# Three weight blocks at a time at the start of seven dense layers, identity products in the norms, and a mean taken later

## The chip, the cores and the metric

The kernel runs on one core of a Trainium2 chip. The metric is the time of one execution on the device, in microseconds (us); where several runs are given, their median. The engines are TensorE (PE; its weight loads PEld), VectorE (DVE), ScalarE (ACT), GpSimd (POOL) and SyncE (SP), whose queue issues most of the loads.

## The reference

Three chains of layers are computed one behind the other on 256 tokens of width 1024 (272 rows where the third chain puts 16 extra tokens ahead). Mixers of several kinds (attention, convolution, state-space and recurrent layers) alternate with dense layers. The dense layer around which the change turns is

```python
def macaron_half_ffn(x, pre_g, post_g, w_gate, w_up, w_down):
    h = rmsnorm(x, pre_g)
    h = (jax.nn.silu(h @ w_gate) * (h @ w_up)) @ w_down
    return x + 0.5 * rmsnorm(h, post_g)
```

with inner width 2816. In the second chain the norm behind a layer is a LayerNorm, which needs a mean and a variance over the 1024 features.

## The kernel before

Activations lie transposed: 8 chunks `k` of 128 features by n tokens. A product with weights is made of three fp32r products of 128x128 by n (L594, L595, L596 in `mm3p`): the weights are split in a high part `wh` (cast on ScalarE, L237) and a low part `wl` (subtraction on VectorE, L238), the activations in `xh` (L253 or L270, ScalarE) and `xl` (L254 or L271, VectorE). Weights come in pieces of 128x1024 fp32 (four rows of chunks by 256 columns) through six raw buffers and five buffers each for `wh` and `wl`. A `get` of eight chunks by 256 columns takes two such pieces.

A dense layer (`ffn`) goes over 11 column blocks `c` of 256. For each it takes a gate and an up block of weights, 8 chunks each. In block 0 of a layer that is not the program's first, gate and up run together per chunk k: 12 matmuls for each chunk, so that TensorE can begin with the first chunk of the normalised input. Then `glu`, and `out_proj` with the down weights: 4 column blocks, each over 22 chunks of the inner width in groups of 8, and for each group first one half of the columns (m = 0), then the other (m = 1). `RmsOut` and `LnOut` take the results, square them (ScalarE: L776, L779, L822) and add the squares up (POOL, L363).

A norm is a place where everything depends on the last result. `add_norm` sums the squares over features with TensorE (`tok_sum`, L295, in parts), makes the reciprocal root of 128x2 numbers in small steps (`inv_sqrt`: L336 or L338 on VectorE, L339 on ScalarE, L340 to L343 on VectorE), broadcasts it with TensorE (`bcast`, L325), scales (L794), adds the residual (L795), and the next layer's `split_x` makes `xh` and `xl`. There are 12 such norms. `layer_norm` (4 of them) does the same with two sums (L866 to L869 take the mean off the variance), two broadcasts and L878 to L880. `hold_weights` sets how many further `get`s may be issued before those whose splits are held back behind the root's steps L339 and L343: after `held` gets the next one waits for both.

`LnOut.late` takes the mean of the first 768 features off before the last two chunks are there, so that the squares need no large terms: a product with ones (L851), a copy (L853), and subtractions on POOL (L854, L855) and VectorE (L857). In `out_proj` it is called for the last column block after the first group of the first half, m = 0.

The order of instructions on each engine is set by a scheduler in the build, which places each instruction by the time it expects for it. So where the source adds an instruction, others move too. Side tasks (the next mixer's inputs, for example) run beside some norms; at others nothing else is there for TensorE.

Of the kernel before, what the change touches and what calls it, by code (L numbers as in the profile page):

```python
# [8 lines left out]
F32 = mybir.dt.float32  # L9
# [11 lines left out]
KD = D // 128  # L21
# [150 lines left out]
def parts_tile(p, name, k, n, dtype=F32R, **kw):  # L172

    return p.tile([128, k, (n + 63) // 64 * 64], dtype, name=name, **kw)[:, :, :n]
# [68 lines left out]
class Ops(Net):  # L243
# [49 lines left out]
    def tok_part(self, ps, a, nt, first, last):  # L293
        for j in range(nt):
            self.nc.tensor.matmul(ps[:, j:j + 1], a[:, j * 128:(j + 1) * 128], self.tab["ones"],  # L295
                                  start=(j == 0 and first), stop=(j == nt - 1 and last), skip_group_check=True)

    def rsqrt(self, v, nt, name="rs"):

        nc = self.nc  # L300
        m = self.tiny.tile([128, nt], F32, name=name + "m")
        y = self.tiny.tile([128, nt], F32, name=name + "y")
        t = self.tiny.tile([128, nt], F32, name=name + "t")
        i = self.tiny.tile([128, nt], I32, name=name + "i")
        nc.vector.tensor_scalar(i, v.bitcast(I32), 1, None, op0=OP.logical_shift_right)
        nc.vector.tensor_scalar(y.bitcast(I32), i, -1, 0x5F3759DF, op0=OP.mult, op1=OP.add)
        nc.vector.tensor_scalar(m, v, -0.5, None, op0=OP.mult)
        for _ in range(3):
            nc.vector.tensor_mul(t, y, y)
            nc.vector.tensor_mul(t, t, m)  # L310
            nc.vector.scalar_tensor_tensor(y, t, 1.5, y, op0=OP.add, op1=OP.mult)
        return y
# [205 lines left out]
    def ffn(self, x, n, g, wg, wu, wd, out, first=None, side=None, stats=None):  # L518

        nc = self.nc
        with self.phase("ffn") as p, ExitStack() as scope:
            px = scope.enter_context(self.phase("ffx", side="right"))
            vt = rb = ahead = wide = None
            if first:
                x.need(0)
                parts = []
                for i, (k, m) in enumerate(((0, 2), (2, 2), (4, 4))):
                    parts.append(wg.get(k, m, 0, 256))  # L530
                    x.need(i + 1)
                ahead = [Pieces(2, [t for q in w for t in (q.tiles[0][:, i:i + 2] for i in range(0, q.each, 2))])
                         for w in zip(*parts)]
                first()
            xh, xl = self.split_x(px, x, n, g)
            hh = parts_tile(p, "hh", FF // 128, n)
            hl = parts_tile(p, "hl", FF // 128, n)
            pair = n <= 256

            def tiles(other=0):  # L540
                if pair:
                    t = self.acc.tile([128, 2, 256], F32, name="acc")
                    return t[:, :, :n], [t[:, m, :n] for m in range(2)]
                t = [(self.acc, self.aux)[m < other].tile([128, 512], F32, name=("acc", "aux")[m < other])[:, None, :n]
                     for m in range(2)]
                return t, [a[:, 0] for a in t]

            def mm(ps, w, k):
                for m in range(2):
                    ms = slice(m * 128, m * 128 + 128)  # L550
                    self.mm3p(ps[m], w[0][:, k, ms], w[1][:, k, ms], xh[:, k], xl[:, k],
                              k == 0 and (m == 0 or not pair), k == KD - 1 and (m == 1 or not pair))

            for c in range(FF // 256):
                cg = ahead if ahead and c == 0 else wg.get(0, KD, c * 256, 256)
                cu = wu.get(0, KD, c * 256, 256)
                tg, pg = tiles(2 * (c == 1))
                tu, pu = tiles(c == 1)
                if c == 0 and not first:
                    for k in range(KD):  # L560
                        mm(pg, cg, k)
                        mm(pu, cu, k)
                else:
                    for k in range(KD):
                        mm(pg, cg, k)
                    for k in range(KD):
                        mm(pu, cu, k)
                if c == 0 and g is not None and n == 256 and stats is None:
                    rb, wide = self.rms_wide(p, x, n)
                elif c == 0 and g is not None:  # L570
                    rt, rb, vt = self.rms(x, stats or n)
                    if side:
                        side.stats = rt, rb
                    rb, vt = rb[:, :n], vt[:, :self.nt(n)]
                    if not pair:
                        self.hold_weights(1)
                if pair:
                    self.glu(p, hh[:, 2 * c:2 * c + 2], hl[:, 2 * c:2 * c + 2], tg, tu, rb, n, 2)
                else:
                    for m in range(2):  # L580
                        i = 2 * c + m
                        self.glu(p, hh[:, i:i + 1], hl[:, i:i + 1], tg[m], tu[m], rb, n, 1)
            o = out(hh[:, FF // 128 - 1, 0:1].bitcast(F32))
            self.out_proj(wd, hh, hl, n, list(range(FF // 128)), o, side=side and (lambda: side.place(px)))
            if side:
                side.scope = scope.pop_all()
            if wide is not None:
                vt = self.by_tokens(wide, n, 1e-6)
            return o, vt
# [25 lines left out]
    def out_proj(self, w, hh, hl, n, ks, out, early=None, side=None):  # L615

        blocks = [ks[i:i + 8] for i in range(0, len(ks), 8)]
        for c in range(KD // 2):
            if c == 1 and side:
                side()  # L620
            if early is not None and c < len(early.open):
                early.rest(c, out)
                continue
            pair = n <= 256 and c < KD // 2 - 1
            if pair:
                t = self.acc.tile([128, 2, 256], F32, name="acc")
                ps = [t[:, m, :n] for m in range(2)]
            else:
                t = [self.acc.tile([128, 512], F32, name="acc")[:, None, :n] for _ in range(2)]
                ps = [a[:, 0] for a in t]  # L630
            for bi, b in enumerate(blocks):
                k0 = min(b)
                assert sorted(b) == list(range(k0, k0 + len(b)))
                wt = w.get(k0, len(b), c * 256, 256)
                for m in range(2):
                    ms = slice(m * 128, m * 128 + 128)
                    for kk, k in enumerate(b):
                        self.mm3p(ps[m], wt[0][:, k - k0, ms], wt[1][:, k - k0, ms], hh[:, k], hl[:, k],
                                  bi == 0 and kk == 0 and (m == 0 or not pair),
                                  bi == len(blocks) - 1 and kk == len(b) - 1 and (m == 1 or not pair))  # L640
                    if bi == 0 and m == 0 and c == KD // 2 - 1 and len(blocks) > 1 and isinstance(out, LnOut):
                        out.late()
                    if bi == len(blocks) - 1 and not pair:
                        out.evac(2 * c + m, t[m])
            if pair:
                out.evac(2 * c, t[:, :, :n])
# [113 lines left out]
class RmsOut:  # L760
# [23 lines left out]
    def add_norm(self, x, g, half, vt, last=False):  # L784
        s, nc, n = self.s, self.s.nc, self.n
        ss = s.tok_sum([self.total[0], self.last], n)
        c, _ = s.inv_sqrt(ss, s.nt(n), 1.0 / D, 1e-6 if vt is None else vt, half)
        s.hold_weights()
        cb = s.bcast(c, n)
        xn = s.xp.tile([128, KD, n], F32, name="x")  # L790

        def make(k):
            t = s.tmp.tile([128, n], F32, name="t")
            nc.vector.scalar_tensor_tensor(t, self.o[:, k], s.col(g, k), cb, op0=OP.mult, op1=OP.mult)  # L794
            (nc.gpsimd if last and k % 2 else nc.vector).tensor_add(xn[:, k], x[:, k, :n], t)  # L795

        return Lazy(xn, make)


class LnOut:  # L800
# [59 lines left out]
    def layer_norm(self, g, b, width=None):  # L860
        s, nc, n, o = self.s, self.s.nc, self.n, self.o
        nt = s.nt(n)
        m1 = s.tok_sum([o[:, 6], o[:, 7]], n)
        s2 = s.tok_sum([self.sum2[0]] + self.squares, n)
        v0, m, mm, mr = (s.tiny.tile([128, nt], F32, name="ln" + k) for k in "0123")
        nc.vector.tensor_scalar(m, m1, 1.0 / D, None, op0=OP.mult)  # L866
        nc.vector.tensor_mul(mm, m, m)
# [2 lines left out]
        r, _ = s.inv_sqrt(v0, nt, 1.0, 0.0)  # L870
# [1727 lines left out]
```

## Time and profile before

| | |
|---|---|
| median of 3 runs | 3132.03 us (3131.13 to 3134.92) |
| profiled execution | 3120.05 us |
| its span, first to last instruction | 3117.8 us |
| TensorE busy | 3009.0 us, 97% |
| VectorE busy | 2071.4 us, 66% |
| ScalarE busy | 1527.8 us, 49% |
| POOL busy | 324.1 us, 10% |
| data read from memory | 487.35 MB, 157 GB/s over the span |

The busy time of TensorE counts matmuls at whatever clock was granted. The rows further down show single places: a timeline row gives when an instruction (or a run of the same ones) started, how long it lasted, its engine and line, what it writes and reads, and in brackets how long the engine was idle before it and what ended that.

### The profile page before, as it was taken

To read this page: it belongs to the slowest core of one execution; us is meant where nothing else is said; L and a number is where in the kernel's file an instruction comes from. 1 tells how busy PE (TensorE), PEld (TensorE's weight loads), DVE (VectorE), ACT (ScalarE), POOL (GpSimd) and SP (SyncE) were. 2 spreads that over 40 slices of the span, in tenths; PEclk is the share of its full clock that TensorE was granted. 3 is DMA by queue.
4 is the path that set the end of the run, shared out by engine and by line. 5 is a ranking of instruction groups with operands and counts; after the bars stand their busy time and mean duration, and the time that the engine had idled before them with its cause. 6 is when DMAs were issued, how large, how long until landed. Compare 5 with 4: busy or idle time off the path is not lost.

```text
span 3117.8 us, 63347 instructions
## 1 busy us (share of the span) xinstructions
PE 3009.0 (97%) x26260; PEld 2899.6 (93%) x26260; DVE 2071.4 (66%) x3465; ACT 1527.8 (49%) x2418; POOL 324.1 (10%) x379
## 2 busy tenths in 40 slices
PE   8999999999899999999999999999999999999998
PEld 8998999999777899999989999999989999998898
DVE  6578766658867765657886665565566656658764
ACT  5455555545433544546565454454444444444543
POOL 0010101000211100001100110100102001012101
PEclk9999999999999999999999999999999999999999
DMA  7664566665311466765345536555443555662453
GB/s 241 192 190 137 167 188 191 203 201 172 103 36 35 123 192 197 208 191 174 112 135 161 171 118 194 180 155 171 142 129 108 172 170 165 193 196 90 130 192 119
DMA packets 142528, 494.61 MB, mean 159 GB/s; under 512 B 15760, under 2 KB 18448, under 8 KB 141984
## 3 DMA queue, kind: packets, MB, share of 16 engines
q1 hardware_dynamic: 136512, 478.88, 49.8%
q10 hardware_dynamic: 5696, 11.62, 1.1%
q8 instruction: 206, 3.38, 0.4%
q14 instruction: 82, 0.67, 0.1%
q0 software_dynamic: 32, 0.07, 0.0%
HBM read 487.35 MB, written 3.15 MB: 157 GB/s over the span
## 4 chain that ended last, share of the span: by engine, by line
PE 90%; DVE 5%; ACT 2%; POOL 2%; issue 1%; DMA 0%; SPq 0%; POOLq 0%; DVEq 0%; ACTq 0%
PE acc L594 25%; PE acc L595 25%; PE acc L596 25%; PE aux L1430 2%; DVE wl L238 1%; PE aux L295 1%; POOL acc L363 1%; PE aux L325 1%; PE acc L2433 1%; ACT wh L237 1%; PE acc L514 1%; PE acc L515 1%; PE acc L516 1%; PE aux L1450 0%; PE aux L668 0%
## 5 line engine op out<-in xcount | busy, mean ns | idle before, releaser
L238 DVE TENSOR_TENSOR wl<-raw,wh 128x1024 fp32r<-128x1024 f32 (+2 forms) x934 | 1123.9, 1207 | 688.4 <-ACT wh L237 679.1
L237 ACT CAST wh<-raw 128x1024 fp32r<-128x1024 f32 (+2 forms) x934 | 952.3, 1023 | 1091.4 <-PE acc L595 802.1
L594 PE MATMUL acc<-xh,wh 128*128 128x256 f32 (+1 forms) x4464 | 1263.8, 285 | 28.9 <-ACT xh L270 17.0
L595 PE MATMUL acc<-xl,wh 128*128 128x256 f32 (+1 forms) x4464 | 1255.1, 282 | 1.3 <-DVE xl L271 1.3
L596 PE MATMUL acc<-xh,wl 128*128 128x256 f32 (+1 forms) x4464 | 1254.8, 281 | 0.9 <-DVE wl L238 0.9
L594 PEld LDWEIGHTS acc<-xh,wh 128*128 128x128 f32 x4464 | 849.6, 191 | 36.7 <-ACT xh L270 18.4
L595 PEld LDWEIGHTS acc<-xl,wh 128*128 128x128 f32 x4464 | 851.7, 191 | 6.5 <-issue 3.6
L596 PEld LDWEIGHTS acc<-xh,wl 128*128 128x128 f32 x4464 | 850.6, 191 | 3.0 <-DVE wl L238 1.3
L594 PE MATMUL acc<-hh,wh 128*128 128x256 f32 (+1 forms) x1760 | 490.2, 279 | 0.0
L596 PE MATMUL acc<-hh,wl 128*128 128x256 f32 (+1 forms) x1760 | 489.8, 278 | 0.0
L595 PE MATMUL acc<-hl,wh 128*128 128x256 f32 (+1 forms) x1760 | 489.8, 278 | 0.0
L595 PEld LDWEIGHTS acc<-hl,wh 128*128 128x128 f32 x1760 | 330.9, 188 | 0.1
L594 PEld LDWEIGHTS acc<-hh,wh 128*128 128x128 f32 x1760 | 330.6, 188 | 0.1
L596 PEld LDWEIGHTS acc<-hh,wl 128*128 128x128 f32 x1760 | 330.6, 188 | 0.0
L363 POOL TENSOR_TENSOR acc<-so 128x256 f32<-128x256 f32 (+1 forms) x16 | 19.6, 1227 | 1120.0 <-ACT so L779 1119.5
L363 POOL TENSOR_TENSOR acc<-acc,so 128x256 f32<-128x256 f32 (+1 forms) x68 | 80.9, 1189 | 305.9 <-ACT so L779 303.1
L607 DVE TENSOR_TENSOR gv<-acc,glu 128x512 f32<-128x512 f32 (+1 forms) x130 | 77.5, 611 | 47.8 <-PE acc L596 42.0
L595 PE MATMUL acc<-ml,wh 128*128 128x256 f32 x280 | 79.8, 287 | 2.3 <-DVE ml L254 2.3
L602 DVE TENSOR_TENSOR glu<-acc,rb 128x512 f32<-128x512 f32 (+1 forms) x106 | 61.3, 596 | 30.4 <-PE acc L596 30.3
L594 PE MATMUL acc<-mh,wh 128*128 128x256 f32 x280 | 80.6, 290 | 0.9 <-ACT mh L1678 0.8
L596 PE MATMUL acc<-mh,wl 128*128 128x256 f32 x280 | 78.9, 284 | 0.0
L609 DVE TENSOR_TENSOR hl<-gv,hh 128x512 fp32r<-128x512 f32 (+1 forms) x132 | 77.2, 602 | 0.0
(620 smaller groups left out, 3772.8 us busy)
## 6 DMA issues: line engine op xcount, KB each, us to landing
raw<-w SPq DMA_DIRECT2D x880, 512.0 KB, 3.9
raw<-w SPq DMA_DIRECT2D x46, 256.0 KB, 3.1
so<-memT ACTq DMA_DIRECT2D x20, 256.0 KB, 3.8
raw<-w SPq DMA_DIRECT2D x8, 192.0 KB, 2.8
x<-xT SPq DMA_DIRECT2D x4, 256.0 KB, 6.1
mk<-so ACTq DMA_DIRECT2D x4, 256.0 KB, 2.5
mv<-so ACTq DMA_DIRECT2D x4, 256.0 KB, 2.9
mk<-mk ACTq DMA_DIRECT2D x1, 1024.0 KB, 4.8
```

Of the source, the lines that this page charges most:

```text
L237: nc.scalar.copy(h, r)
L238: nc.vector.tensor_sub(l, r, h.bitcast(F32))
L295: self.nc.tensor.matmul(ps[:, j:j + 1], a[:, j * 128:(j + 1) * 128], self.tab["ones"], start=(j == 0 and first), stop=(j == nt - 1 and las ...
L325: self.nc.tensor.matmul(ps[:, j * 128:j * 128 + w], r[:w, j:j + 1].to_broadcast([w, 128]), self.tab["ident"][:w, :w], start=(j == 0), stop ...
L363: self.nc.gpsimd.tensor_add(d, total[1], t)
L594: t.matmul(out, wh, xh, start=first, stop=False, **kw)
L595: t.matmul(out, wh, xl, start=False, stop=False, **kw)
L596: t.matmul(out, wl, xh, start=False, stop=last, **kw)
L602: nc.vector.tensor_mul(s, pg, rb[:, None, :].to_broadcast([128, m, n]))
L607: nc.vector.tensor_mul(v, pu, s)
L609: nc.vector.tensor_sub(hl, v, hh.bitcast(F32))
L1430: nc.tensor.matmul(ps[R[a], c], lhsT(c, a), rhs(c, a), start=first and c == 0, stop=c == 3, skip_group_check=True)
```

## The change

Three edits are made.

In `ffn`, in seven layers (those with n <= 256 that are not the program's first), the start takes three weight blocks at a time: gate 0, up 0 and gate 1 (columns 256 on). They are got as pieces of four chunks, and each chunk is used for 18 matmuls instead of 12; block 1 then has only its up block to run. Where `held` is 2 it becomes 5 there: with gets of one piece that makes five pieces which may be split before the norm's root, where it was four (two gets of two).

`run_on(count)` issues products of the 128x128 identity with itself in fp32, into an unused PSUM tile: 5 behind the token sum of `add_norm`, 8 behind those of `layer_norm`. Each shows as two matmul records. 92 products are added in all.

`out.late()` is called after m = 1 instead of m = 0, 24 matmuls further on, in the two dense layers with a LayerNorm behind them.

```diff
+    def run_on(self, count):
+
+        ps = self.aux.tile([128, 512], F32, name="aux")
+        for _ in range(count):
+            self.nc.tensor.matmul(ps[:, :128], self.tab["ident"], self.tab["ident"], start=True, stop=True)
...
+            three = pair and not first
+            if three and self.held == 2:
+                self.held = 5
             for c in range(FF // 256):
-                cg = ahead if ahead and c == 0 else wg.get(0, KD, c * 256, 256)
-                cu = wu.get(0, KD, c * 256, 256)
-                tg, pg = tiles(2 * (c == 1))
-                tu, pu = tiles(c == 1)
-                if c == 0 and not first:
+                if three and c == 0:
+
+                    each = [(wg, 0), (wu, 0), (wg, 256)]
+                    got = [[w.get(k, 4, at, 256) for w, at in each] for k in (0, 4)]
+                    both = [[Pieces(4, [a[i].tiles[0], b[i].tiles[0]]) for i in range(2)] for a, b in zip(*got)]
+                    (tg, pg), (tu, pu), ahead1 = [tiles() for _ in range(3)]
+                    for k in range(KD):
+                        for w, ps in zip(both, (pg, pu, ahead1[1])):
+                            mm(ps, w, k)
+                elif three and c == 1:
+                    cu = wu.get(0, KD, 256, 256)
+                    (tg, pg), (tu, pu) = ahead1, tiles()
+                    for k in range(KD):
+                        mm(pu, cu, k)
...
-                    if bi == 0 and m == 0 and c == KD // 2 - 1 and len(blocks) > 1 and isinstance(out, LnOut):
+                    if bi == 0 and m == 1 and c == KD // 2 - 1 and len(blocks) > 1 and isinstance(out, LnOut):
                         out.late()
...
         ss = s.tok_sum([self.total[0], self.last], n)
+        s.run_on(5)
...
         s2 = s.tok_sum([self.sum2[0]] + self.squares, n)
+        s.run_on(8)
```

The order of the instructions changes around the norms. Lines of the changed kernel are numbered further on: from L325 on 6 more, from L594 on 26 more, from L784 on 26 or 27 more. Names: `so`, `acc` squares, `o` the layer's result, `isv`, `isr`, `isy`, `ist`, `isc` the steps of the reciprocal root, `wh` and `wl` the parts of a weight piece, `tab_all` the table that holds ones and the identity. A row ending in x2 stands for two instructions in succession.

The norm near 1046 us, ScalarE. Before:

```order
L779 ACTIVATE so<-acc 128x512
L779 ACTIVATE so<-acc 128x256
L237 CAST wh<-raw 128x1024
L776 ACTIVATE acc<-acc 128x256
L409 CAST one<-tab_all 128x128
L339 ACTIVATE isr<-isv 128x2
L237 CAST wh<-raw 128x1024
L270 ACTIVATE xh_13339<-x,vec 128x256
```

After:

```order
L805 ACTIVATE so<-acc 128x512
L805 ACTIVATE so<-acc 128x256
L237 CAST wh<-raw 128x1024 x2
L802 ACTIVATE acc<-acc 128x256
L415 CAST one<-tab_all 128x128
L345 ACTIVATE isr<-isv 128x2
L270 ACTIVATE xh_13369<-x,vec 128x256
```

The second cast L237 has moved from behind the root (L339, now L345) to ahead of the last square (L776, now L802).

The same norm, VectorE. Before:

```order
L782 COPY o<-acc 128x512
L782 COPY o<-acc 128x256
L238 TENSOR_TENSOR wl<-raw,wh 128x1024
L782 COPY o<-acc 128x256
L336 TENSOR_SCALAR isv<-aux 128x2
L340 RECIPROCAL isy<-isr 128x2
L341 TENSOR_TENSOR ist<-isy 128x2
L342 SCALAR_TENSOR_TENSOR ist<-ist,isv 128x2
L343 SCALAR_TENSOR_TENSOR isc<-ist,isy 128x2
L238 TENSOR_TENSOR wl<-raw,wh 128x1024
L794 SCALAR_TENSOR_TENSOR t<-o,vec,aux 128x256 x2
```

After:

```order
L808 COPY o<-acc 128x512
L808 COPY o<-acc 128x256
L238 TENSOR_TENSOR wl<-raw,wh 128x1024 x2
L808 COPY o<-acc 128x256
L342 TENSOR_SCALAR isv<-aux 128x2
L346 RECIPROCAL isy<-isr 128x2
L347 TENSOR_TENSOR ist<-isy 128x2
L348 SCALAR_TENSOR_TENSOR ist<-ist,isv 128x2
L349 SCALAR_TENSOR_TENSOR isc<-ist,isy 128x2
L821 SCALAR_TENSOR_TENSOR t<-o,vec,aux 128x256 x2
L822 TENSOR_TENSOR x<-x,t 128x256 x2
```

The second split L238 has moved from behind the root's last step (L343, now L349) to ahead of its first (L336, now L342).

The LayerNorm near 1836 us, TensorE. Before:

```order
L596 MATMUL acc<-oh,wl 128x256
L295 MATMUL aux<-tab_all,o 128x1 x2
L295 MATMUL aux<-tab_all,acc 128x1 x2
L295 MATMUL aux<-tab_all,so 128x1 x8
L295 MATMUL aux<-tab_all,sq 128x1 x2
L295 MATMUL aux<-tab_all,o 128x1 x2
L295 MATMUL aux<-tab_all,sq 128x1 x2
L325 MATMUL aux<-tab_all,isc 128x128 x2
L325 MATMUL aux<-tab_all,ln_22768 128x128 x2
L594 MATMUL acc<-xh_22797,wh 128x256 x3
```

After:

```order
L622 MATMUL acc<-oh,wl 128x256
L295 MATMUL aux<-tab_all,o 128x1 x2
L295 MATMUL aux<-tab_all,acc 128x1 x2
L295 MATMUL aux<-tab_all,so 128x1 x8
L295 MATMUL aux<-tab_all,sq 128x1 x2
L302 MATMUL aux<-tab_all 128x128 x2
L295 MATMUL aux<-tab_all,o 128x1 x2
L302 MATMUL aux<-tab_all 128x128 x5
L295 MATMUL aux<-tab_all,sq 128x1 x2
L302 MATMUL aux<-tab_all 128x128
L331 MATMUL aux<-tab_all,isc 128x128 x2
L331 MATMUL aux<-tab_all,ln_22831 128x128 x2
L620 MATMUL acc<-xh_22860,wh 128x256 x3
```

Eight identity products (L302) have come in: two ahead of the sum over the last two chunks of the result, five ahead of the sum of the last squares, one behind it.

## Rows read from the trace of the kernel before

**Rows 1.** Page, part 1, and the answer on cores (span, mean granted clock).
```profile
PE 3009.0 (97%) x26260; PEld 2899.6 (93%) x26260; DVE 2071.4 (66%) x3465; ACT 1527.8 (49%) x2418; POOL 324.1 (10%) x379
...
core 0: 3117.8 us, clock 0.979
```

**Rows 2.** What TensorE waited for: us, times, longest us.
```profile
PE aux L325 <- DVE isc L343: 17.5, 13, 2.2
PE acc L594 <- ACT xh L270: 17.0, 8, 2.4
...
PE aux L851 <- POOL acc L363: 3.5, 3, 1.5
PE aux L295 <- POOL acc L363: 3.2, 3, 1.5
...
PE aux L295 <- ACT acc L776: 0.5, 1, 0.5
```

**Rows 3.** Timeline, norm near 1046: start, length, engine, line, operation, [idle <-releaser].
```profile
1045.03 0.38 ACT L776 ACTIVATE acc<-acc 128x256 f32<-128x256 f32 x1 [0.42 <-PE acc L596]
...
1045.46 0.52 PEld L295 LDWEIGHTS aux<-tab_all,acc 128*128 128x128 f32 x4 [0.22 <-ACT acc L776]
...
1046.12 0.15 DVE L336 TENSOR_SCALAR isv<-aux 128x2 f32<-128x2 f32 x1
...
1046.41 1.03 ACT L237 CAST wh<-raw 128x1024 fp32r<-128x1024 f32 x1
...
1047.34 0.71 PE L325 MATMUL aux<-tab_all,isc 128*128 128x128 f32 x4 [1.27 <-DVE isc L343]
1047.47 1.23 DVE L238 TENSOR_TENSOR wl<-raw,wh 128x1024 fp32r<-128x1024 f32 x1 [0.18 <-ACT wh L237]
1048.62 0.87 DVE L794 SCALAR_TENSOR_TENSOR t<-o,vec,aux 128x256 f32<-128x256 f32 x2
...
1050.41 0.80 PE L594 MATMUL acc<-xh,wh 128*128 128x256 f32 x2 [2.36 <-ACT xh L270]
```

**Rows 4.** Windows after it: busy us (instructions) by engine, clock, DMA share, GB/s.
```profile
1050.20:1053.60 3.40, 3.19 (x15) 3.19 (x16) 3.40 (x10) 2.37 (x7) 1.75 (x2) 0.52 0.32 123
1053.60:1057.00 3.40, 3.40 (x31) 3.40 (x31) 3.40 (x8) 1.96 (x6) 2.46 (x4) 0.98 0.02 5
```

**Rows 5.** Timeline of TensorE, two broadcasts back to back near 1430.
```profile
1429.35 0.60 PE L325 MATMUL aux<-tab_all,isc 128*128 128x128 f32 x4
1429.79 0.61 PE L325 MATMUL aux<-tab_all,ln 128*128 128x128 f32 x4
```

**Rows 6.** Timeline of TensorE, LayerNorm near 1758.
```profile
1759.57 0.59 PE L295 MATMUL aux<-tab_all,sq 128*128 128x1 f32 x4
1761.64 1.22 PE L325 MATMUL aux<-tab_all,isc 128*128 128x128 f32 x4 [1.49 <-DVE isc L343]
1762.65 1.06 PE L325 MATMUL aux<-tab_all,ln 128*128 128x128 f32 x4
```

**Rows 7.** Timeline, the later half of a LayerNorm layer: the late mean.
```profile
1409.72 0.70 PE L851 MATMUL aux<-acc,tab_all 128*128 128x256 f32 x2 [1.46 <-POOL acc L363]
...
1410.94 3.56 DVE L857 TENSOR_TENSOR o<-o,rb 128x512 f32<-128x512 f32 x3 [1.86 <-ACT rb L853]
```

**Rows 8.** Timeline of TensorE, layer near 2614: side sum over tokens.
```profile
2627.37 0.83 PE L295 MATMUL aux<-tab_all,acc 128*128 128x1 f32 x6 [0.99 <-POOL acc L363]
```

**Rows 9.** Timeline of TensorE, LayerNorm near 1836: last part of the sum.
```profile
1837.67 0.99 PE L295 MATMUL aux<-tab_all,sq 128*128 128x1 f32 x4
```

**Rows 10.** Timeline of TensorE, first matmul behind three norms with side work.
```profile
530.00 0.62 PE L594 MATMUL acc<-xh,wh 128*128 128x256 f32 x3 [1.96 <-ACT xh L270]
...
1240.46 0.50 PE L594 MATMUL acc<-xh,wh 128*128 128x256 f32 x2 [1.03 <-ACT xh L253]
...
1434.42 0.39 PE L514 MATMUL acc<-wh,xh 128*128 128x256 f32 x1 [2.96 <-ACT xh L253]
```

**Rows 11.** Window around the norm near 1240.
```profile
1238.00:1246.00 8.00, 6.96 (x59) 6.60 (x58) 7.20 (x20) 4.35 (x10) 0.00 (x0) 1.00 0.49 153
```

More of the change, by code (lines that the diff above doesn't have):

```diff
@@ L552, in mm @@
                               k == 0 and (m == 0 or not pair), k == KD - 1 and (m == 1 or not pair))
+            three = pair and not first
+            if three and self.held == 2:
+                self.held = 5
             for c in range(FF // 256):
-                cg = ahead if ahead and c == 0 else wg.get(0, KD, c * 256, 256)
-                cu = wu.get(0, KD, c * 256, 256)
-                tg, pg = tiles(2 * (c == 1))
-                tu, pu = tiles(c == 1)
-                if c == 0 and not first:
+                if three and c == 0:
[11 more added lines that the diff above has]
+                        mm(pu, cu, k)
+                else:
+                    cg = ahead if ahead and c == 0 else wg.get(0, KD, c * 256, 256)
+                    cu = wu.get(0, KD, c * 256, 256)
+                    tg, pg = tiles(2 * (c == 1))
+                    tu, pu = tiles(c == 1)
+                if three and c < 2:
+                    pass
+                elif c == 0 and not first:
                     for k in range(KD):
```

## The prediction

> **What bounds the kernel now.** I read the page first. TensorE is busy 97% of the span, and the mean granted clock is 0.979 [rows 1]. The clock has two levels, 1.2 and 2.4 GHz, so a mean of 0.979 over 3117.8 us means 2 x 0.021 x 3117.8 = 131 us at the lower one, and at most half of that, 65 us, lost by it. The list of what TensorE waited for comes second: its largest entries are the wait for a norm's reciprocal root (13 times, 17.5 us) and for the first normalised chunk (8 times, 17.0 us); the late mean costs 3.5 us in three waits [rows 2]. So the kernel is a stream of matmuls, interrupted at its 16 norms, and the edits work only there.
>
> The timeline of one norm without other work beside it, the one near 1046 us, shows how such a place is built [rows 3]. TensorE ends the projection and sums squares over tokens (L295). It waits 0.22 us for ScalarE's last square (L776); that is the norm's first wait, since the second half of the sum needs it. Then L336 starts at 1046.12 and five small steps on VectorE and ScalarE follow, while TensorE idles 1.27 us before the broadcast L325. Then L794, L795 and the split of the first chunk follow, and TensorE idles 2.36 us more before L594 at 1050.41. VectorE also runs a weight split (L238) at 1047.47, which ends at 1048.70, and L794 starts only at 1048.62 although the broadcast ended at 1048.05: that split costs the norm about 0.5 us. The clock reads 0.52 in the 3.4 us after the restart, 0.98 in the 3.4 us after those, and TensorE is busy without a pause there: 31 matmuls in 3.40 us, 0.11 us each [rows 4]. So the price of a norm is three waits plus some 3.4 x 0.48 = 1.6 us of slow clock. The supply of chunks does not limit TensorE once it has restarted.
>
> **Price of an identity product.** The trace has no such product, but the broadcast has the same shape and type: two products show as four records. Where broadcasts run back to back, the second begins 1429.79 - 1429.35 = 0.44 us after the first [rows 5], hence 0.22 us a product; at the lower clock 1762.65 - 1761.64 = 1.01, hence 0.50 [rows 6]. Five cost 1.1 us (2.5 slow), eight 1.8 (4.0 slow). What is left to find is where they stand in TensorE's order and whether TensorE had a wait there.
>
> **The later mean.** L851 follows the POOL sum L363 and held TensorE for 1.46 us [rows 7]; the same happened at 2015, and the list gives that as the longest of three [rows 2]. The change puts it 24 matmuls later, 24 x 0.11 = 2.6 us, which covers 1.46. Behind it POOL and VectorE have the mean to subtract (VectorE's part takes 3.56 us [rows 7]) and the squares follow; they are wanted at the token sum, about 85 matmuls, 9.4 us, later. So I take 2 x -1.46 = **-2.9 us**; if half comes back at the next norm, -1.5.
>
> **Three blocks where a dense layer begins, and five pieces held.** Seven layers do it. 18 matmuls a chunk instead of 12 give the chunks more time, 2.0 us against 1.3 at full clock, but [rows 4] leave no wait to remove, so I take 0 for the matmuls. The order of the loads on SP's queue is unchanged, and on POOL two rows change places, so nothing is added there. What moves is the fifth piece of weights. Before, its cast (L237, 1.03 us) stands behind the norm's root on ScalarE and its split (L238, 1.23 us) on VectorE between the root's end and L794. After, the cast stands ahead of the last square and the split ahead of L336. At the norms near 334, 1046 and 2920 us nothing else runs beside this. The cast needs a buffer that the projection's second-last matmul frees, so it runs from about 1044.95 to 1045.98 and the square starts 0.95 us later than 1045.03; the split then ends about 1047.2, and L336 starts about 1.3 us later than 1046.12. Against it stand the 0.5 us of the split that is gone ahead of L794: +0.8 to +0.9 each, and the five products (1.1 us) fit into that longer first wait. **+2.7 us** for three; from +1.2 (the norm near 2920 waits for a POOL sum anyway, up to 1.5 us by [rows 2]) to +4.2, if the 0.5 does not come back. ScalarE works in the order of its queue, so behind that cast wait the square, the root and every chunk.
>
> A gain at the layer near 2614: a side sum over tokens waited 0.99 us for POOL [rows 8]. It stands 69 matmuls, 7.6 us, later in the new order, so **-1.0** (0 if POOL moves with it).
>
> **Products at the LayerNorms.** Eight products each. At the norm near 1430 they take the place of side matmuls ahead of a wait for the first chunk that is 2.96 us long [rows 10]: 0. At those near 1758 and 1836 no wait stands where they are put. L295 runs from part to part, the last part starts 1759.57 and directly follows the others [rows 6], and seven of the eight stand ahead of it. So 7 x 0.22 = 1.55 is added at full clock, 3.5 at the lower one, which the second of them shows: four records of L295 in 0.99 us instead of 0.59 [rows 9]. The split moved ahead of the root there runs beside the products. I take 1.6 and 2.0, **+3.6** (1.0 to 7.0). At the third, near 2031, seven of eight stand ahead of the last part too, with some small waits beside them: **+1.0** (0 to 1.6).
>
> **Products at the other norms.** At those near 530 and 1240 they fall ahead of waits for a chunk of 1.96 and 1.03 us [rows 10]: 0. At three norms with matmuls of a side task between the sum and the broadcast (near 195, 730 and 2801) TensorE has no wait there, so up to 1.1 each is added, less whatever is waiting later: **+1.5** for the three (0 to 3.3). At the norm near 2402 the first wait is 0.5 [rows 2], so +0.6; at the last one two products stand between the sum's parts with nothing to wait for, +0.4: together **+1.0** (0 to 1.6). Near 2240 and 2612 two and three products stand between the parts: **+0.5** (0 to 1.4).
>
> **The clock.** The edits leave the two waits behind the root at every norm, and [rows 3, 4] show that these two are followed by low clock. On the other hand one norm, near 1240, has a single wait of 1.03 us and no low stretch: its 8 us read 1.00 [rows 10, 11]. Where a norm has a short second wait, products in the first may suffice; I take one stretch of low clock fewer in all, **-1.6** (none to three, 0 to -5).
> The Trainium skill, "TensorE: Matmul & The Clock Gate", section "Why this matters for your kernels", says that it is long idle gaps between bursts of matmuls that drop the clock. By that rule the products would change nothing about the clock, since no wait at a norm without side work is longer than 2.4 us, and the sum would be without the -1.6. The trace does not bear the rule out: the clock fell at 1050 after waits of 0.2, 1.27 and 2.36 us [rows 3, 4].
>
> **Sum.** -2.9 + 2.7 - 1.0 + 3.6 + 1.0 + 1.5 + 1.0 + 0.5 - 1.6 = +4.8 us. The profiled execution took 3120.05 us, so 3124.9 by its own time; the median of the runs is 3132.03, 12 us above it, and the same 4.8 us give **3137**. With the bounds, leaving out that all fall on one side, -2 to +12: 3130 to 3144.
>
> **Rivals.** First, *the clock holds* (faster). The first wait gets work of TensorE's, and if that keeps the clock up behind most norms, the gain is 1.6 us a norm; at 6 to 14 of the 16 norms that is 10 to 22 us, less the +6.4 of the other terms: -4 to -16, 3116 to 3128. Then the wider first step would matter too, since at full clock 12 matmuls take a chunk in 1.3 us, near the pace at which VectorE's steps per chunk (L794, L795, L271) deliver. It decides from the point where the two waits that remain, 1.27 and 2.36 us with 0.72 of broadcast between, no longer lower the clock. Against it speaks [rows 4], for it [rows 11]. Beside it stands the Trainium skill's section "A second HAM failure mode: psum-queue depth-cycling" on the same page: frequent short idles are enough to make the clock swing. That agrees with 0.52 after three short waits, and filling one of the three is what the change does.
> Second, *the cast and the products lengthen the norms* (slower). If the cast ahead of the last square delays seven norms rather than three, 7 x 1.3 = 9, and the products at the LayerNorms run at the lower clock, 7 + 1.6, the sum is 9 + 8.6 + 2 - 2.9 = +17, and a slow stretch more at one or two places makes +18 to +20: 3150 to 3152. For it: [rows 3] show how close to the end of the projection these steps stand.
> Third, *the products are hidden everywhere and the blocks change nothing*: only the later mean remains, -3 to 0: 3129 to 3132.
>
> **Chances.** My sum 0.56, the clock holds 0.23, longer norms 0.13, only the mean 0.08. A difference of 0.2%, 6.3 us, is about the least that can be told from none. My sum's range lies for the greater part within it: of its 0.56 some 0.30 is within and 0.26 slower. The first rival is faster in 0.20 and within in 0.03; the second is slower; the third is within. Faster 0.20, same 0.41, slower 0.39. The range that holds 8 in 10 reaches into the first and second rival: 3118 to 3149.
>
> **What would show it.** In the changed profile TensorE's waits on L851 should lose 2.9 us. Near 1046 the identity products should end before the last square, and L336 start about 1.3 us later after the projection's end than before, with L794 directly behind the broadcast. Near 1758 the time from the first L295 to L325 should grow by 1.6 us or more. The mean clock should stay at 0.979 to 0.981; at 0.985 or above the first rival is right. The forecast is wrong if the wait for the root (L325) shrinks at the lone norms, or if products stand at half clock where I count them at full.

## The result, and the profile after

The changed kernel took 3165.66 us in the median of four runs (3162.79 to 3173.27), beside 3133.48 us for the kernel before (four runs as well); the ratio is 1.0107, with a 95% interval from 1.0082 to 1.0132. It is slower by about 34 us. The forecast was 3137 with a range that ended at 3149, so it was wrong: it had named a loss, but one that can hardly be told from none.

The page of the profiled execution (span; busy time of each engine, share, instructions), and the answer on cores:

```profile
span 3160.8 us, 63719 instructions
...
PE 3050.1 (96%) x26444; PEld 2940.9 (93%) x26444; DVE 2067.6 (65%) x3465; ACT 1526.0 (48%) x2418; POOL 327.5 (10%) x379
```

```profile
core 0: 3160.8 us, clock 0.977
```

The span has grown by 43.0 us over [rows 1], TensorE's busy time by 41.1. The clock's mean has gone down a little, 0.979 to 0.977. What TensorE waited for (us, times, longest us):

```profile
PE acc L620 <- ACT xh L270: 16.2, 10, 2.3
PE aux L331 <- DVE isc L349: 15.3, 14, 1.8
PE acc L620 <- DVE glu L628: 12.6, 4, 3.2
...
PE aux L295 <- POOL acc L369: 3.2, 4, 1.5
...
PE aux L878 <- POOL acc L369: 0.6, 1, 0.6
```

Against [rows 2], the wait on the mean's product fell from 3.5 to 0.6 us, as forecast, and that for the root from 17.5 to 15.3. A group has come that [rows 2] do not have at all: 12.6 us in four waits for `glu`, the scaling of the gate (L628, which was L602).

Where the 43 us arose is read by matching the k-th product with weights of one trace with the k-th of the other. The lag grows by 5.43, 5.32, 5.43 and 5.59 us within the 250 products that hold each of these four waits, 21.8 us in all. It grows by 1.11 us for every 250 products through nearly the whole dense layer that the kernel before runs from 1240 to 1423 us, 6.7 us, though no wait stands there. Another 4.9 us arise near 250 us, in a mixer, where the low clock lasted longer. These are not the change's: the second trace of the kernel before, the last of the three lines below, has the same 4.9 us over its first. The same window in the kernel before, the changed kernel and the kernel before again (busy us of PE, PEld, DVE, ACT, POOL with their instructions, granted clock, DMA share, GB/s):

```profile
242.00:260.00 18.00, 16.58 (x114) 13.18 (x113) 13.46 (x55) 13.05 (x37) 0.00 (x0) 0.91 0.42 147
```

```profile
242.00:260.00 18.00, 18.00 (x91) 15.82 (x90) 9.94 (x33) 7.91 (x18) 0.00 (x0) 0.62 0.50 174
```

```profile
242.00:260.00 18.00, 18.00 (x93) 15.58 (x93) 8.55 (x34) 9.70 (x26) 0.00 (x0) 0.62 0.43 147
```

What is left, 9.6 us, lies at the norms, the mean and the other mixers.

The first of the four places, TensorE (L416 is the sum of squares over features; start, length, and in brackets the idle time and what ended it):

```profile
364.63 0.28 PE L416 MATMUL aux<-th,one 128*128 128x256 f32 x1
...
374.02 0.35 PE L620 MATMUL acc<-xh,wh 128*128 128x256 f32 x1 [3.22 <-DVE glu L628]
```

VectorE in the same stretch:

```profile
365.59 0.42 DVE L419 TENSOR_SCALAR rw<-aux 128x256 f32<-128x256 f32 x1
...
367.06 1.74 DVE L423 RECIPROCAL rb<-t 128x256 f32<-128x256 f32 x1
368.72 1.16 DVE L238 TENSOR_TENSOR wl<-raw,wh 128x1024 fp32r<-128x1024 f32 x1
...
370.13 1.22 DVE L238 TENSOR_TENSOR wl<-raw,wh 128x1024 fp32r<-128x1024 f32 x1
...
372.06 1.22 DVE L238 TENSOR_TENSOR wl<-raw,wh 128x1024 fp32r<-128x1024 f32 x1
373.19 1.28 DVE L628 TENSOR_TENSOR glu<-acc,rb 128x512 f32<-128x512 f32 x2
```

The sum over features is followed by a chain on VectorE: L419, a reciprocal (L423), L424 to L426, then the scaling L628, which reads the accumulator of the first gate block and so is the first step to give it back. Four weight splits (L238) stand in between. From L416 to L628 it takes 8.6 us. Only 5.4 us of matmuls (block 1's up part, 48 products) are left for TensorE by then, and at 370.80 it stands still for 3.22 us. In the kernel before, TensorE and then VectorE:

```profile
351.78 0.28 PE L410 MATMUL aux<-th,one 128*128 128x256 f32 x1
```

```profile
354.88 1.75 DVE L417 RECIPROCAL rb<-t 128x256 f32<-128x256 f32 x1
...
360.01 1.28 DVE L602 TENSOR_TENSOR glu<-acc,rb 128x512 f32<-128x512 f32 x2
```

There the chain took about as long, 8.2 us, but it began after 96 products; another 96, 10.8 us, followed before the next block needed the accumulator. The wait has a sequel. Windows of the changed kernel (columns as above):

```profile
370.80:374.00 3.20, 0.00 (x1) 0.01 (x1) 3.20 (x7) 2.05 (x3) 0.00 (x0) 1.00 0.75 223
374.20:377.60 3.40, 3.40 (x18) 3.40 (x18) 2.26 (x4) 1.56 (x3) 0.00 (x0) 0.53 0.70 236
377.60:381.00 3.40, 3.40 (x31) 3.40 (x31) 1.34 (x2) 1.57 (x2) 0.00 (x0) 0.97 0.02 7
```

A single wait of 3.2 us is followed by 3.4 us at a clock of 0.53, 18 products instead of 31: another 1.4 to 1.6 us. Wait and slow clock make up 4.6 to 4.8 of the 5.4 us; the rest is not resolved.

### The profile page after: what moved, and what is told of

It is laid out like the page before. It is cut to its first block, busy times and chain, and to the rows that moved or that the text cites. A ratio compares the mean times of both kernels' runs of the same rounds, so it can differ in the third digit from the quotient of the medians.

```text
span 3160.8 us, 63719 instructions
## 1 busy us (share of the span) xinstructions
PE 3050.1 (96%) x26444; PEld 2940.9 (93%) x26444; DVE 2067.6 (65%) x3465; ACT 1526.0 (48%) x2418; POOL 327.5 (10%) x379
## 4 chain that ended last, share of the span: by engine, by line
PE 88%; DVE 6%; ACT 2%; issue 2%; POOL 1%; DMA 0%; SPq 0%; POOLq 0%; DVEq 0%; ACTq 0%
PE acc L620 25%; PE acc L621 25%; PE acc L622 24%; PE aux L1458 2%; DVE wl L238 2%; PE aux L295 1%; PE aux L302 1%; PE aux L331 1%; PE acc L2461 1%; ACT wh L237 1%; POOL acc L369 1%; PE acc L520 1%; PE acc L521 1%; PE acc L522 1%; PE aux L1478 0%
## 5 line engine op out<-in xcount | busy, mean ns | idle before, releaser
L238 DVE TENSOR_TENSOR wl<-raw,wh 128x1024 fp32r<-128x1024 f32 (+2 forms) x934 | 1125.3, 1210 | 728.7 <-ACT wh L237 719.8
L237 ACT CAST wh<-raw 128x1024 fp32r<-128x1024 f32 (+2 forms) x934 | 950.0, 1023 | 1113.1 <-PE acc L621 811.2
L628 DVE TENSOR_TENSOR glu<-acc,rb 128x512 f32<-128x512 f32 (+1 forms) x106 | 61.2, 596 | 29.8 <-PE acc L622 29.7
```

What stands on the lines that cost most here:

```text
L237: nc.scalar.copy(h, r)
L238: nc.vector.tensor_sub(l, r, h.bitcast(F32))
L628: nc.vector.tensor_mul(s, pg, rb[:, None, :].to_broadcast([128, m, n]))
```

## The experiments

Three theories were set against each other. **A**: in four layers the longer first step delays the sum over features, as above. **B**: the third open block takes an accumulator that a later block needs. **C**: the loss is in the norms, by the products, the earlier cast and the clock. Each kernel was timed beside the kernel before on the same chip; the ratios are to that. In some stretches TensorE needs 117.7 ns a product and in others 113.3, at the same granted clock of 1.00, and which stretches these are varies from execution to execution (last section). So a trace's span is also given less the time that this slow pace cost in it.

**The later mean alone** (m == 0 becomes m == 1 in the kernel before).

```diff
-                    if bi == 0 and m == 0 and c == KD // 2 - 1 and len(blocks) > 1 and isinstance(out, LnOut):
+                    if bi == 0 and m == 1 and c == KD // 2 - 1 and len(blocks) > 1 and isinstance(out, LnOut):
```

> The kernel before with the later mean alone. All theories: the two waits of 1.46 us on the mean's product go and nothing comes back, -2.9 us, so a ratio of 0.999. If half of it comes back at the LayerNorm behind, -1.5 us.

Measured: 3134.1 us, ratio 1.0007 (0.9981 to 1.0033). The wait is gone, as TensorE's timeline shows; no idle time is put ahead of L851:

```profile
1416.16 0.59 PE L851 MATMUL aux<-acc,tab_all 128*128 128x256 f32 x2
```

A gain of 2.9 us lies within the interval, and so does none. The trace tells more. Against the kernel before, the lag falls by 1.8 us at each of the two places, and rises by 4.3 and 1.9 us at the two LayerNorms behind them, near 1430 and 2031. At the second, the start of the token sum in the kernel before and then here:

```profile
2028.60 0.50 PE L295 MATMUL aux<-tab_all,o 128*128 128x1 f32 x4
2028.97 0.58 PE L295 MATMUL aux<-tab_all,acc 128*128 128x1 f32 x4
```

```profile
2035.43 0.61 PE L295 MATMUL aux<-tab_all,o 128*128 128x1 f32 x4 [0.74 <-DVE o L832]
2036.76 1.01 PE L295 MATMUL aux<-tab_all,acc 128*128 128x1 f32 x4 [0.71 <-POOL acc L363]
```

Two waits of 0.7 us have come in, for VectorE's last part of the result (L832) and for POOL's sum of squares, which both stand behind the mean's subtractions, and the sum goes on at the lower clock (1.01 us for four records, not 0.58). Near 1430 the same two waits have come in, 0.74 and 0.71 us, and the window behind them reads a clock of 0.50:

```profile
1430.00:1436.00 6.00, 6.00 (x30) 6.00 (x30) 2.76 (x11) 2.98 (x5) 0.00 (x0) 0.50 0.43 140
```

**The identity products alone** (`run_on` and its two calls in the kernel before).

```diff
...
+        s.run_on(5)
...
+        s.run_on(8)
```

> The kernel before with the 92 identity products alone. In the profile of the changed kernel the 16 norms together cost about 19 us more than before, with the earlier cast and split in that. Theory A (the loss is mainly in the dense layers' start) expects the products alone to cost 8 to 14 us. Theory C (the products and what stands around them in the norms are the main loss) expects 20 us or more, and the clock below 0.979.

Measured: 3142.3 us, ratio 1.0032 (1.0007 to 1.0056), about 10 us: A's size. Its waits and clock:

```profile
PE acc L600 <- ACT xh L270: 16.6, 10, 2.4
PE aux L331 <- DVE isc L349: 10.3, 12, 1.4
```

```profile
core 0: 3126.6 us, clock 0.984
```

The wait for the root fell from 17.5 to 10.3 us, and the clock rose from 0.979 to 0.984 in this trace (0.980 to 0.984 in the ten runs, against 0.977 to 0.981 for the kernel before). So the products do hold the clock, and part of their time is hidden, but the rest costs more than the clock gives.

**The three-block start alone**, with five pieces held.

```diff
+            three = pair and not first
+            if three and self.held == 2:
+                self.held = 5
...
```

> The kernel before with the three weight blocks and the five held pieces alone, no products and the mean where it was. Theory A: four layers make a sum of squares over features with TensorE, and the program puts it behind the first step, so that it comes after 144 matmuls and not 96; the scale of the gate and with it the accumulators come free 3.2 us too late, and 3.4 us of slow clock follow: 4 x 5.4 = 22 us, with the earlier cast some 24. Theory C: about +5 us.

Measured: 3159.3 us, ratio 1.0078 (1.0053 to 1.0103), 24 us: A's number, against 5 by C. The list of waits has the same four on `glu`, 12.6 us.

**The changed kernel with the sum earlier**, once and once more on a chip beside the changed kernel.

```diff
                     for k in range(KD):
                         for w, ps in zip(both, (pg, pu, ahead1[1])):
                             mm(ps, w, k)
+                        if k == 5 and g is not None and n == 256 and stats is None:
+                            rb, wide = self.rms_wide(p, x, n)
...
```

> The changed kernel with one thing moved: in the four layers the sum of squares over features is issued after six of the eight chunks of the first step, 108 matmuls and not 144. Theory A: the four waits of 3.2 us for the gate's scaling go, and the slow clock behind them: 3165.7 - 22 = 3144 us. Rival B (it is the third open block, which takes an accumulator that the third gate block needs): the waits stay, 3166 us.

> The changed kernel, unchanged, with more runs: 3166 us and a ratio of 1.011 as in its first four runs. The four waits of 3.2 us on the gate's scaling stand at the same places; the layers at the slower pace are others than in its first trace, if the pace is drawn.

> The changed kernel with the sum of squares after 108 matmuls, again, on the same chip as the changed kernel. Theory A: 20 to 24 us faster than the changed kernel in the mean of the runs; its first runs gave only some 10, with three more layers at the slower pace in its trace. Rival B: the same time.

Measured: the first time 3156.2 us, ratio 1.0074 (1.0047 to 1.0102), which by itself decides little between A's 3144 and B's 3166. The second time 3151.1 us, ratio 1.0051 (1.0020 to 1.0082), beside the changed kernel with 3164.2, ratio 1.0113 (1.0076 to 1.0149): 13 us, less than the 20 to 24 of A. The traces are more definite. The largest three of the second run:

```profile
PE acc L623 <- ACT xh L270: 15.9, 10, 2.0
PE aux L331 <- DVE isc L349: 14.9, 14, 1.8
PE acc L623 <- ACT wh L237: 6.7, 1, 6.7
```

No wait for `glu` is left, with the same accumulators and the same three blocks open. The sum and the scaling there, TensorE and VectorE:

```profile
362.43 0.28 PE L416 MATMUL aux<-th,one 128*128 128x256 f32 x1
```

```profile
367.95 1.28 DVE L631 TENSOR_TENSOR glu<-acc,rb 128x512 f32<-128x512 f32 x2
```

The scaling starts 5.5 us behind the sum, with one split in between and not four, and TensorE does not wait. Within the 250 products that hold each of the four places the lag over the kernel before grows by 0.0 to 0.1 us in this trace, where the changed kernel had 5.3 to 5.6. That rules B out. In the spans, 3160.8 and 3157.2 us for the changed kernel stand against 3160.5 and 3140.9; but less the slow pace they are 3140.9 and 3144.9 against 3120.9 and 3121.9, 20 and 23 us, as A says, and less the longer low clock near 250 us, which differs between these traces too, 17 and 19. That the times show only 10 and 13 us has a possible reason in the pace: of the eight dense layers with 256 columns four, one and four run at the slower one in the three traces with the early sum (the next experiment has the third), and one, none and one in the three with the three-block start and the late sum. Whether the early sum brings this about or chance does, three traces of each do not tell.

**The three-block start with the earlier sum, alone.**

> The three-block start and five held pieces alone, as in the kernel that took 3159 us, with the sum of squares over features issued after 108 matmuls and not 144. Theory A: the four waits on the gate's scaling go: 3159 - 22 = 3137 us; what is left over the kernel before, 3 to 6 us, is the earlier cast and split. Rival B (a third open accumulator): 3159 us.

Measured: 3141.6 us, ratio 1.0025 (0.9996 to 1.0054), against 1.0078 with the late sum: 0.53% or 17 us (on two chips, each against the kernel before on the same one), and 24 us in the spans less the slow pace (3137.5 and 3113.7). A again.

**The changed kernel without the three-block start.**

> The changed kernel without the three-block start: identity products and later mean, starts of 12 matmuls a chunk and four held pieces. Theory A (the start's late sum is the main loss): 3166 - 24 = 3142 us or less, the products' +11 and the mean's -3 giving 3139. If the parts work on each other, so that the products cost more only together with the longer start, it comes to 3131 or less.

Measured: 3140.0 us, ratio 1.0052 (1.0021 to 1.0083). The median is A's 3139. By the ratio it is some 16 us above the kernel before, where A's 3139 means 8; the interval holds that, and it does not hold 3131. The two halves, 0.52% and 0.78%, come to a little more than the whole's 1.07% and 1.13%, within the intervals.

**Earlier sum, four pieces held, later mean, no products.**

```diff
-                self.held = 5
+                self.held = 4
...
```

> The three-block start with the early sum, four held pieces as before the change, the later mean, no products. Theory A with the cast's price: 3137 - 3 - 3 = 3131 us, level with the kernel before; near 1046 us the first step of the root starts no later after the projection than in the kernel before (1.29 us). If it is faster by more than 0.2% (under 3125), the wider start is a gain in itself.

Measured: 3134.0 us, ratio 1.0014 (0.9992 to 1.0036): level with the kernel before, no faster. So no gain of a wider start in itself is to be seen, which fits [rows 4], where the chunks did not limit TensorE. Near 1046 us the root's first step starts 1.29 us after the projection again and the first chunk's product 5.58 us after it, both as in the kernel before; the three-block start alone, with five pieces held and no products, has 2.64 and 6.42.

**Twice the products** (10 and 16).

> The kernel before with twice the identity products (10 and 16 at a norm, 184 in all), nothing else. If a product costs its own time where no wait covers it, the second half finds none and costs 92 x 0.22 = 20 us less what the clock gives: 3150 to 3162 us. If instead the products' cost is the pace at which TensorE goes on after them, about the same as with 92: 3140 to 3146 us.

Measured: 3146.6 us, ratio 1.0061 (1.0029 to 1.0093), between the two expectations, and the interval takes in both. The trace's span less the slow pace went up by 18.5 us over that with 92 products (3126.3 against 3107.8), but 4.7 us of this are the longer low clock near 250 us, so some 14 of the 20 us that 92 products take at full clock were added. The wait for the root is down to 5.0 us, and the clock of the ten runs is 0.983 to 0.988. The times show less: the medians of the two kernels differ by 4 us and the ratios by 9, and the intervals overlap.

**The kernel before again.**

> The kernel before, unchanged, for a second trace of it. If the pace of a dense layer's matmuls (113.3 or 117.7 ns each at a granted clock of 1.00) is drawn anew in each execution, other layers run at the slower pace than in its first trace, where one layer in the third chain began to; if it belongs to the program, the same ones do.

Measured: 3125.2 us in a single run. The table counts, for each trace, the products of 256 columns that began 116 to 119.5 ns after the one before them, at full clock, and what they cost over 113.3 ns each.

| trace | span | slow products | cost | span less cost |
|---|---|---|---|---|
| kernel before | 3117.8 | 2317 | 10.1 | 3107.7 |
| kernel before, again | 3123.0 | 2517 | 11.0 | 3112.0 |
| changed | 3160.8 | 4504 | 19.9 | 3140.9 |
| changed, again | 3157.2 | 2805 | 12.3 | 3144.9 |
| later mean | 3123.7 | 3750 | 16.5 | 3107.2 |
| products | 3126.6 | 4235 | 18.8 | 3107.8 |
| three blocks | 3154.7 | 3886 | 17.2 | 3137.5 |
| changed, early sum | 3160.5 | 8905 | 39.6 | 3120.9 |
| changed, early sum, again | 3140.9 | 4305 | 19.0 | 3121.9 |
| no three blocks | 3134.9 | 4114 | 18.3 | 3116.6 |
| three blocks, early sum | 3151.3 | 8457 | 37.6 | 3113.7 |
| four held | 3129.4 | 3793 | 16.8 | 3112.6 |
| products doubled | 3164.1 | 8490 | 37.8 | 3126.3 |

The last column still holds each trace's share of slow clock, so a few microseconds there say nothing. The longer low clock near 250 us alone is up to 4.9 of them: against the first trace of the kernel before it is 0 to 0.6 us in the later mean, the products and the second early sum, 2.1 in the first early sum, and 4.7 to 4.9 in all the others.

## Why the prediction was wrong, point by point

**The three-block start: the step that failed.** The prediction had the edits work "only there", at the norms, and took "0 for the matmuls", since [rows 4] show no wait behind the restart. That answered whether chunks limit TensorE, and the answer holds: the early sum with four pieces held is level. What I did not ask is who waits for the *end* of the first step. The sum over features stands behind it in four of the seven layers; 48 products later means 5.4 us later for it, for the chain of 8 us on VectorE, and for the accumulators. I had read 351.78 to 360.01 us in the trace of before and not set it against the 10.8 us that TensorE then had left, a margin of 2 us once the first half of the scaling is done. Its price is the measured lag, four times some 5.4 us (that this is also the length of 48 products is chance), 21.8 us, of the 29 by which the forecast was short. That this is the cause is shown three ways: the part alone has the four waits and the loss, and the early sum removes the waits and the lag at these places, with the rest of the change and without it. Its size is less sure in the times: early against late sum gave 10, 13 and 17 us there.

**The later mean: the wait right, the gain not.** 3.5 to 0.6 us of waiting, as forecast. But the prediction let at most half of the 2.9 us come back at the next norm, and by the traces about all of it does. In the seven traces with the later mean the two waits gain 3.7 to 4.1 us together, and at the two LayerNorms behind them, near 1430 and 2031, the lag over the kernel before grows by 3.8 to 6.1 us together. In the five without it, the kernel before again among them, it grows there by 0.0 and 0.6 us at the most.

**The earlier cast and split: right.** The norm near 1046, in the changed kernel:

```profile
1062.62 0.50 PE L295 MATMUL aux<-tab_all,acc 128*128 128x1 f32 x4
...
1062.98 1.36 PE L302 MATMUL aux<-tab_all 128*128 128x128 f32 x10
...
1063.65 0.38 ACT L802 ACTIVATE acc<-acc 128x256 f32<-128x256 f32 x1
...
1065.26 0.15 DVE L342 TENSOR_SCALAR isv<-aux 128x2 f32<-128x2 f32 x1
...
1066.48 0.71 PE L331 MATMUL aux<-tab_all,isc 128*128 128x128 f32 x4 [1.79 <-DVE isc L349]
1067.23 0.87 DVE L821 SCALAR_TENSOR_TENSOR t<-o,vec,aux 128x256 f32<-128x256 f32 x2 [0.80 <-PE aux L331]
...
1069.04 1.01 PE L620 MATMUL acc<-xh,wh 128*128 128x256 f32 x3 [1.84 <-ACT xh L270]
```

and the start of its token sum in the kernel before:

```profile
1044.83 1.24 PE L295 MATMUL aux<-tab_all,acc 128*128 128x1 f32 x8
```

The projection's end is where L295 starts: 1044.83 there, 1062.62 in the changed kernel. L342 starts 2.64 us after it against 1.29 for L336, so 1.35 later (forecast 1.3). The products are issued from 1062.98 and end at 1064.34, by about 0.3 us behind the last square (1063.65 to 1064.03) where the forecast had them ahead of it; L821 starts directly behind the broadcast. The first chunk's product comes 6.42 us after the projection against 5.58, so 0.84 later (0.8 to 0.9 forecast). With four pieces held both delays are gone (above), so they are the cast's and the split's. The wait for the root did not shrink here in the full change (1.27 to 1.79 us).

**Products at the LayerNorms: the mechanism right, the size not.** Near 1758, in the changed kernel and then in the one before:

```profile
1787.55 0.61 PE L295 MATMUL aux<-tab_all,o 128*128 128x1 f32 x4 [0.35 <-DVE o L859]
...
1790.69 3.15 PE L302 MATMUL aux<-tab_all 128*128 128x128 f32 x14
...
1796.42 0.71 PE L331 MATMUL aux<-tab_all,isc 128*128 128x128 f32 x4 [1.28 <-DVE isc L349]
...
1800.23 1.01 PE L620 MATMUL acc<-xh,wh 128*128 128x256 f32 x3 [2.66 <-ACT xh L253]
```

```profile
1755.88 0.61 PE L295 MATMUL aux<-tab_all,o 128*128 128x1 f32 x4 [0.35 <-DVE o L832]
...
1765.65 1.01 PE L594 MATMUL acc<-xh,wh 128*128 128x256 f32 x3 [1.93 <-ACT xh L253]
```

From the first part of the sum to the first chunk it took 9.77 us and now takes 12.68, 2.9 more, where I took 1.6. The seven products are the difference: 2.94 us from 1790.69 to the next part at 1793.63, 0.42 each and not 0.22, because most ran at the lower clock (0.54 from 1790.70 to 1793.60). Near 1836 it is 3.4 instead of 2.0. Both lie under the upper bound that the prediction carried (3.5 each); I took the price of full clock for a place at which the sums alone do not keep the clock up. Near 1430 and 2031, forecast at 0 and +1.0, the lag grew by 2.7 and 2.4 us, but with the products alone it did not grow at all; that growth is the later mean's, above. The smaller terms at the other norms were not tested one by one.

**The clock.** I counted one stretch of slow clock fewer. The products alone do raise the mean clock, so the first rival has its mechanism; but its gain stayed below their cost (ratio 1.0032, and 1.0061 with twice as many). In the full change the mean fell (0.977 in the trace, 0.974 to 0.977 in the runs), as the four new waits each bring their own slow stretch. The second rival named a loss of the right sign and put it at the norms. A part of it is there: without the three-block start the loss is 0.52%. The larger part is not: that start alone loses 0.78%.

## What to carry to other kernels

When a first step is made longer, list what is issued behind it in the same engine's order and what that work releases; the extra length is a delay for all of it, and a slack of 2 us in the old order is the number to compare with. A wait taken away where it stands is a gain only if the next place at which everything meets does not take it back. Filler work on a busy engine is free only inside a wait, and where the clock is low it costs double (0.42 us a product here, not 0.22). One trace is one draw: compare traces instruction by instruction before a difference of spans is put down to an edit.

## What was not expected of the hardware

TensorE has two paces at the same granted clock. The same 50 us of a dense layer in the kernel before, the changed kernel and the changed kernel again (same columns as the windows above):

```profile
1300.00:1350.00 50.00, 50.00 (x444) 50.00 (x443) 27.81 (x28) 23.75 (x28) 0.00 (x0) 1.00 0.66 194
```

```profile
1300.00:1350.00 50.00, 50.00 (x427) 50.00 (x426) 27.94 (x28) 23.45 (x27) 0.00 (x0) 1.00 0.62 186
```

```profile
1300.00:1350.00 50.00, 50.00 (x443) 50.00 (x443) 28.64 (x28) 24.21 (x29) 0.00 (x0) 1.00 0.65 194
```

All three read a clock of 1.00 and a TensorE without pause, but 427 products fit in the second and 443 or 444 in the others: from start to start 117.8 ns on average against 113.3. A layer of 1,584 products costs 7 us more at the slower pace. In the 13 traces each of the eight dense layers with 256 columns has one pace for 86% of its products or more (the two with 272 columns take 123.3 ns in all of them). A change stands where the stream was interrupted (a norm, a product in plain fp32, a wait), though in a mixer, near 764 us in the kernel before, the pace changed within an unbroken stream as well. It is not the program's alone, since the changed kernel had this layer at the slower pace in one trace and not in the other, and the early sum had three layers differ between its two traces. Whether it is wholly free is open: in both traces of the kernel before none of these eight layers runs at the slower pace. What decides it was not found. It may be why runs of one kernel spread over 30 us, and why the first measurement of the early sum showed half of its gain; that is argued from one trace a run, not shown.
